# Attention in a hybrid diffusion step: key sums taken in the columns of the output, divisions on output rows

## The chip, the cores and the metric

The kernel runs on one core of a Trainium2 chip. The metric is device time in microseconds for one launch. The engines named below are TensorE (PE; its weight loads are listed apart as PEld), VectorE (DVE), ScalarE (ACT), GpSimd (POOL) and SyncE (SP), which issues the DMA transfers. The engines run at the same time and wait for each other through semaphores; each takes its own instructions in order.

## What is computed

The reference is one step of a network of two layers. Each layer projects 1,152 tokens (128 of a prompt, 1,024 of a sample), runs three mixers beside each other, merges them and adds the result to the stream. The change lies in the first mixer, an attention with 8 heads; a key has 64 plain and 32 rotary components, a value 64:

```python
def mla_attention(q_nope, q_rope, k_nope, k_rope, v):
    scale = (QK_NOPE + QK_ROPE) ** -0.5
    def block(qs):
        qn, qr = qs
        s = (jnp.einsum('bqhd,bkhd->bhqk', qn, k_nope)
             + jnp.einsum('bqhr,bkr->bhqk', qr, k_rope)).astype(jnp.float32) * scale
        pr = jax.nn.softmax(s, axis=-1).astype(v.dtype)
        return jnp.einsum('bhqk,bkhd->bqhd', pr, v)
    ...
```

The sample's 1,024 queries attend to 1,152 keys (128 of the context and their own 1,024), the prompt's 128 queries to 128 keys. All data are 32-bit floats.

## The kernel before

Most of a layer is put in order by a planner. The attention (`attn_all`, line 1221) is not: its order is written by hand, as a loop over slots. A **group** is one head with 512 of the sample's queries, 16 groups a layer; groups 16 and 17 hold four heads of the prompt each. A **slot** is one block of 128 keys of one group, nine slots a group, one for a prompt group.

- `st` (in a slot): three products give the scores of 128 keys by 512 queries, keys on partitions, in a PSUM tile st. The query tile q has a row 96 with the negated maximum of each query, against a row of ones in K, so that the maximum is subtracted by the product itself. ScalarE takes the exponential into a tile P. GpSimd adds up the nine P of a group in a tile acc.
- `s1`: the maxima are found ahead, some 18 slots before the group. Twelve products s a group (in the prompt four) have 128 queries on partitions and 384 keys in columns, in two PSUM buffers; VectorE takes the maximum of each (mx), and `rows_a` the maximum of three and its negative (nm, 128 x 4). `rows_b` moves nm by DMA into row 96 of q. In the sample, product t takes the queries t, t + 4, t + 8 and so on, so that a partition's four values of nm lie beside each other in the row and one transfer moves them all; in the prompt it takes 128 queries in a row, and there are four transfers.
- `pv`, three slots behind a group's last block: nine value products (tile po), V as weights, 64 columns by 512 queries. Even blocks add up in PSUM partitions 0 to 63, odd ones in 64 to 127, and go through the two column halves of the array. `fin_b` copies one half to SBUF on ScalarE (tile ot), `fin_e` adds the other on VectorE.
- `fin_a`, one slot later: four products with columns t, t + 4, ... of acc as weights and one column of ones give the sum over keys of each query, with queries on partitions (sm, 128 x 4). VectorE takes the reciprocal (rc), and SP stores it to DRAM (Rd). `fin_c` loads it back, spread over 64 partitions (rb), and `fin_d`, seven slots after `pv`, multiplies ot by rb and stores it (oD).
- For the last three groups `fin_a` and `fin_c` go another way: GpSimd multiplies the identity by rc, and a product with ones spreads the row.

Fill tiles (fg), products of a later gate projection, stand in the beginning of the attention, among its last slots and behind it. Behind them begins the merge of the next stage (tile mg).

Of the kernel before, what the change touches and what calls it, by code (L numbers as in the profile page):

```python
# [8 lines left out]
F32 = mybir.dt.float32  # L9
# [258 lines left out]
class Kern:  # L268
# [101 lines left out]
    def run(self, ctx):  # L370
# [21 lines left out]
        self.Rd = dram("Rd", (18, 512))  # L392
# [828 lines left out]
    def attn_all(self, l):  # L1221
# [19 lines left out]
        def prep(i):  # L1241
# [4 lines left out]
            if hh >= 0:  # L1246
# [11 lines left out]
                stores = [(self.oD[0, hh // 2, r64(hh), t0:t0 + 512], slice(0, 512))]  # L1258
            else:
# [17 lines left out]
                stores = [(self.oD[0, 2 * w:2 * w + 2, r64(h), 0:128].rearrange("j p t -> p j t"), h) for h in range(2)]  # L1277
# [76 lines left out]
        def fin_a(i):  # L1354
            d = groups[i]
            sm = self.psm.tile([128, 512], F32, tag="ms", name=f"sm{d['nm']}")
            for t in range(4):
                self.mm(sm[:, t:t + 1], d["acc"][:, t::4], self.ones[:, 0:1])
            r = self.S("rc", d["nm"], 4)
            nc.vector.reciprocal(r, sm[:, 0:4])  # L1360
            nm = f"rb{d['nm']}"
            if i < NG - 3:
                d["rb"] = pt.tile([128, 512], F32, tag="rb", bufs=1, name=nm)
                self.st(self.Rd[i].rearrange("(x t) -> x t", t=4), r)
            else:
                d["rb"] = pt.tile([128, 512], F32, tag="P", bufs=13, name=nm)
                self.tt("p", d["rb"].rearrange("p (x t) -> p x t", t=4), self.ident.unsqueeze(2).to_broadcast([128, 128, 4]),
                        r.unsqueeze(1).to_broadcast([128, 128, 4]), ALU.mult)

        def fin_b(i):  # L1370
            d = groups[i]
            d["t"] = pt.tile([64, 512], F32, tag="ot", bufs=3, name=f"ot{d['nm']}")
            self.cp("a", d["t"], d["po"][0:64, :] if d["prompt"] else d["po"][64:128, :])

        def fin_e(i):
            d = groups[i]
            if not d["prompt"]:
                self.tt("v", d["t"], d["po"][0:64, :], d["t"], ALU.add)

        def fin_c(i):  # L1380
            d = groups[i]
            if i < NG - 3:
                self.ld(d["rb"][0:64], self.Rd[i].unsqueeze(0).to_broadcast([64, 512]))
                d["rb"] = d["rb"][0:64]
            else:

                rb = self.pst.tile([128, 512], F32, tag="st", name=f"rb{d['nm']}")
                self.mm(rb[0:64, :], self.ones[:, 0:64], d["rb"])
                d["rb"] = rb[0:64]

        def fin_d(i):
            d = groups[i]
            self.tt("v", d["t"], d["t"], d["rb"], ALU.mult)
            for dst, c in d["stores"]:
                self.st(dst, d["t"][:, c] if not d["prompt"] else d["t"].rearrange("p (j h t) -> p j h t", j=2, h=2)[:, :, c])
# [3 lines left out]
        F0, RB, FA, LAG, FC, FD, FE = 18, 2, 1, 3, 3, 6, 2  # L1399
# [36 lines left out]

        for i in range(3):
            add(NS + 1 + i, fin_a, NG - 3 + i)
# [49 lines left out]
        for n in range(NS + 14):  # L1488
# [6 lines left out]
            if x:  # L1495
                if x[1] == groups[x[0]]["blocks"] - 1:
                    pv(x[0])
                    add(n + 1, fin_b, x[0])
                    add(n + FE, fin_e, x[0])
                    if x[0] < NG - 3:  # L1500
                        for f, m in ((fin_a, FA), (fin_c, FA + FC), (fin_d, FA + FD)):
                            add(n + m, f, x[0])
                    else:
                        add(n + 1, fin_c, x[0])
                        add(n + 2, fin_d, x[0])
# [812 lines left out]
```

## Time and profile before

| | |
|---|---|
| median of three runs | 3682.22 us |
| lowest and highest | 3678.1 and 3687.41 us |
| the profiled execution | 3702.81 us |
| its span, first to last instruction | 3701.0 us |
| mean granted TensorE clock | 0.957 |
| TensorE, VectorE, ScalarE, GpSimd busy | 96%, 53%, 30%, 38% |

A page lists busy time and instructions for each engine. A timeline row gives the start, the time until the end of the last of the merged instructions, the engine, the source line (L95 and L98 are helpers through which all instructions go, so tiles tell them apart), the operation with its tiles as output<-inputs, and in brackets how long the engine was idle before and what released it. A 32-bit product that is not in the faster 32-bit format counts as two instructions in the trace: four key sums are eight.

### The profile page before, as it was taken

Reading aid. Unit: us, or ns where it says so; the run is one execution under the profiler, and the core shown is the slowest. Engines: PE = TensorE matmul, PEld = TensorE weight load, DVE = VectorE, ACT = ScalarE, POOL = GpSimd, SP = SyncE. Lnnn points to the kernel's source line nnn. Section 1 sums busy time; section 2 is a strip of 40 time slices with the busy share of each in tenths; the row PEclk is TensorE's granted clock in tenths of the full one; section 3 lists DMA queues with packets and bytes.
Section 4 is the critical chain, followed back from the end, with each engine's and each line's share of the span. In section 5 each row is a group of like instructions: output and inputs, shape, how many; then the busy total and the mean of one; then the engine's idle time right before and its main releaser. Section 6 shows DMA issues by size and latency. Waiting matters only on the chain. (4 is left out here: it accounts for less than half of the span.)

```text
span 3701.0 us, 62464 instructions
## 1 busy us (share of the span) xinstructions
PE 3543.0 (96%) x24330; PEld 3080.1 (83%) x24330; DVE 1969.5 (53%) x4492; ACT 1102.2 (30%) x2327; POOL 1396.8 (38%) x1456
## 2 busy tenths in 40 slices
PE   7999999998999999999999999999999999999998
PEld 4988777777876789999999877777887667999998
DVE  4477676755555234541575777776455542131236
ACT  4432222224233222221344232212242332121234
POOL 3165555432266401332122645653323662123311
PEclk8999899999998899999999989999999998999999
DMA  5332212225622133441233222311364222132222
GB/s 184 93 106 74 57 54 72 68 59 171 185 66 67 47 111 113 121 127 52 101 101 95 87 75 79 77 48 55 98 223 117 69 61 67 56 95 61 81 79 88
DMA packets 315207, 336.79 MB, mean 91 GB/s; under 512 B 146208, under 2 KB 231904, under 8 KB 314528
## 3 DMA queue, kind: packets, MB, share of 16 engines
q1 hardware_dynamic: 314912, 332.80, 30.6%
q8 instruction: 192, 3.15, 0.3%
q14 instruction: 103, 0.84, 0.1%
HBM read 240.16 MB, written 92.47 MB: 90 GB/s over the span
## 5 line engine op out<-in xcount | busy, mean ns | idle before, releaser
L98 PE MATMUL ip<-h,wh_wi 128*128 128x384 f32 x5328 | 1167.0, 358 | 2.3 <-DVE gb L98 1.1
L98 PEld LDWEIGHTS ip<-h,wh_wi 128*128 128x128 f32 x5328 | 933.0, 194 | 54.4 <-issue 15.9
L98 PE MATMUL mg<-h,wh_mg 128*128 128x384 f32 x3456 | 623.2, 335 | 2.5 <-ACT mt L98 2.5
L98 PEld LDWEIGHTS mg<-h,wh_mg 128*128 128x128 f32 x3456 | 602.0, 188 | 3.1 <-ACT mt L98 3.1
L95 POOL TENSOR_TENSOR acc<-acc,P 128x512 f32<-128x512 f32 x224 | 290.2, 1295 | 199.7 <-ACT P L95 188.0
L95 DVE TENSOR_REDUCE mx<-s 128x1 f32<-128x384 f32 (+1 forms) x400 | 206.8, 540 | 240.4 <-PE s L95 239.3
L98 PE MATMUL pp<-ob,wp 128*128 128x384 f32 x1728 | 329.2, 341 | 2.3 <-DVE mU L98 1.2
L98 POOL TENSOR_TENSOR tmp<-M,X 128x2 f32<-128x2 f32 (+30 forms) x310 | 217.7, 702 | 277.1 <-DVE X L98 258.2
L98 PEld LDWEIGHTS pp<-ob,wp 128*128 128x128 f32 x1728 | 305.9, 191 | 11.1 <-DVE mt L98 6.6
L95 PE MATMUL st<-q,K 97*128 97x512 f32 (+1 forms) x912 | 290.4, 434 | 0.0
L95 ACT ACTIVATE P<-st 128x512 f32<-128x512 f32 x292 | 174.5, 598 | 351.4 <-PE st L95 314.7
L98 POOL TENSOR_TENSOR wh_mg<-wrm,wh_mg 128x512 fp32r<-128x512 f32 x88 | 117.1, 1333 | 424.0 <-ACT wh_mg L98 353.5
L98 POOL TENSOR_TENSOR mU<-mU,mt 128x384 f32<-128x384 f32 x96 | 108.3, 1128 | 327.2 <-DVE mt L98 327.1
L95 PEld LDWEIGHTS st<-q,K 97*128 97x128 f32 x912 | 185.1, 215 | 42.7 <-issue 24.3
L98 POOL TENSOR_TENSOR wh_wi<-wri,wh_wi 128x512 fp32r<-128x512 f32 x112 | 153.4, 1380 | 160.0 <-ACT wh_wi L98 157.9
L98 PE MATMUL wop<-mh,wh_wo 128*128 128x384 f32 x1152 | 203.6, 336 | 3.4 <-DVE mt L98 3.4
L98 PEld LDWEIGHTS wop<-mh,wh_wo 128*128 128x128 f32 x1152 | 199.8, 188 | 5.1 <-DVE mt L98 4.0
L98 DVE TENSOR_REDUCE X<-tmp 128x1 f32<-128x2 f32 (+30 forms) x620 | 184.5, 319 | 31.3 <-POOL tmp L98 23.4
L98 DVE SCALAR_TENSOR_TENSOR mt<-mt,pp 128x384 f32<-128x384 f32 x96 | 53.1, 553 | 254.5 <-ACT mt L98 239.9
L98 ACT ACTIVATE VT<-pv,sst 128x64 f32<-128x64 f32 x256 | 66.7, 311 | 367.0 <-DVE scr L98 350.7
L98 DVE TENSOR_TENSOR tmp<-M,X 128x2 f32<-128x2 f32 (+30 forms) x310 | 163.0, 526 | 20.9 <-POOL M L98 15.0
L98 ACT ACTIVATE mt<-mg 128x384 f32<-128x384 f32 x144 | 70.3, 488 | 339.9 <-PE mg L98 329.7
(302 smaller groups left out, 5104.5 us busy)
## 6 DMA issues: line engine op xcount, KB each, us to landing
wri<-in_w_in SPq DMA_DIRECT2D x160, 256.0 KB, 3.4
wrm<-in_w_in SPq DMA_DIRECT2D x96, 256.0 KB, 3.0
wada<-in_w_ada SPq DMA_DIRECT2D x64, 256.0 KB, 3.0
or<-oD SPq DMA_DIRECT2D x72, 192.0 KB, 3.0
wrp<-in_w_p SPq DMA_DIRECT2D x48, 256.0 KB, 3.0
gD<-gt SPq DMA_DIRECT2D x48, 192.0 KB, 1.9
KNd<-hl_uk SPq DMA_DIRECT2D x24, 384.0 KB, 3.4
QNd<-hl_uq SPq DMA_DIRECT2D x24, 384.0 KB, 3.7
```

The costliest lines, as they stand in the source:

```text
L95: return real(*a, **kw)
L98: op.f = lambda: real(*a, **kw)
```

## The change

- The four products for the key sums become two, behind the value products in `pv`: 64 columns of ones as weights, 256 queries of acc in columns. The first writes PSUM partitions 0 to 63, the second 64 to 127, so that each sum stands on 64 partitions, in the place of the output row that it divides.
- The output tile ot becomes 128 x 256: queries 0 to 255 on partitions 0 to 63, queries 256 to 511 on 64 to 127. Copies and additions are made in two halves; there are two stores a group.
- `fin_d` takes the reciprocal of 128 x 256 in PSUM and multiplies. It is called just before the next group's `pv`; for the last three groups two slots after their own.
- `fin_a`, `fin_c`, the tile in DRAM and GpSimd's products with the identity are gone.
- The two halves for value blocks are swapped: even blocks now use partitions 64 to 127.
- Product t of the maxima takes 128 queries in a row also in the sample; `rows_b` makes four transfers for every group.

```diff
-            ts = slice(t * 128, t * 128 + 128) if d["prompt"] else slice(t, 512, 4)
+            ts = slice(t * 128, t * 128 + 128)
 def rows_b(i):
-            if d["prompt"]:
-                for t in range(4):
-                    self.ld(row[:, t * 128:t * 128 + 128], mr[:, t:t + 1])
-            else:
-                self.ld(row, mr)
+            for t in range(4):
+                self.ld(row[:, t * 128:t * 128 + 128], mr[:, t:t + 1])
 def pv(i):
-            for b in range(n if n > 1 else 0):
-                self.mm(po[b % 2 * 64:b % 2 * 64 + 64, :], Vs[i][:, b], d["P"][b], b < 2, b > n - 3)
+            else:
+                for b in range(n):
+                    h = (b + 1) % 2 * 64
+                    self.mm(po[h:h + 64, :], Vs[i][:, b], d["P"][b], b < 2, b > n - 3)
+            if i < NG - 2:
+                d["sm"] = self.psm.tile([128, 512], F32, tag="ms", name=f"sm{d['nm']}")
+            else:
+                d["sm"] = self.pst.tile([128, 512], F32, tag="st", name=f"sm{d['nm']}")
+            for h in range(2):
+                self.mm(d["sm"][h * 64:h * 64 + 64, 0:256], self.ones[:, 0:64], d["acc"][:, h * 256:h * 256 + 256])
-        def fin_a(i):
-            for t in range(4):
-                self.mm(sm[:, t:t + 1], d["acc"][:, t::4], self.ones[:, 0:1])
-            nc.vector.reciprocal(r, sm[:, 0:4])
-            if i < NG - 3:
-                self.st(self.Rd[i].rearrange("(x t) -> x t", t=4), r)
-            else:
-                self.tt("p", d["rb"]..., self.ident..., r..., ALU.mult)
...
 def fin_b(i):
-            d["t"] = pt.tile([64, 512], F32, tag="ot", bufs=3, name=f"ot{d['nm']}")
-            self.cp("a", d["t"], d["po"][0:64, :] if d["prompt"] else d["po"][64:128, :])
+            t, po = pt.tile([128, 256], F32, tag="ot", bufs=3, name=f"ot{d['nm']}"), d["po"]
+            self.cp("a", t[0:64], po[0:64, 0:256] if d["prompt"] else po[64:128, 0:256])
+            self.cp("a", t[64:128], po[0:64, 256:512])
 def fin_e(i):
-                self.tt("v", d["t"], d["po"][0:64, :], d["t"], ALU.add)
+                self.tt("v", t[0:64], po[0:64, 0:256], t[0:64], ALU.add)
+                self.tt("v", t[64:128], po[64:128, 256:512], t[64:128], ALU.add)
 def fin_d(i):
-            self.tt("v", d["t"], d["t"], d["rb"], ALU.mult)
+            nc.vector.reciprocal(sm, sm)
+            self.tt("v", t, t, sm, ALU.mult)
 main loop, at a group's last block, three slots behind
+                    if 0 < i < NG - 2:
+                        fin_d(i - 1)
                     pv(x[0])
```

On TensorE, from the last value product of group 1 on, before (po value products, st scores, s products for the maxima, sm key sums; the numbers in names are those of group, block and buffer):

```order
L95 MATMUL po_1_10625<-P_1_8_10576,V_0_10151 64x512
L95 MATMUL st_2_3_10635<-q_2_10046,K_1_10049 128x512 x3
L95 MATMUL s_4_4_10642<-K_2_10050,q_0_10044 128x384
L95 MATMUL s_4_5_10645<-K_2_10050,q_0_10044 128x384
L95 MATMUL sm_1_10650<-cst,acc_1_1_10473 128x1 x4
L95 MATMUL st_2_4_10659<-q_2_10046,K_1_10049 128x512 x3
```

The same place on TensorE after the change:

```order
L95 MATMUL po_1_10633<-P_1_8_10579,V_0_10150 64x512
L95 MATMUL sm_1_10643<-acc_1_1_10478,cst 64x256 x2
L95 MATMUL st_2_3_10646<-q_2_10045,K_1_10048 128x512 x3
L95 MATMUL s_4_4_10653<-K_2_10049,q_0_10043 128x384
L95 MATMUL s_4_5_10656<-K_2_10049,q_0_10043 128x384
L95 MATMUL st_2_4_10662<-q_2_10045,K_1_10048 128x512 x3
```

The sums moved ahead of a slot's scores and of two products for the maxima, right behind the value products.

On VectorE, around the value products of group 1, which TensorE starts after product s_4_3, before:

```order
L95 TENSOR_SCALAR nm_3_10589<-mx_3_10234 128x4
L95 TENSOR_REDUCE mx_4_10465<-s_4_0_10591 128x1
L95 TENSOR_REDUCE mx_4_10465<-s_4_1_10594 128x1
L95 TENSOR_TENSOR ot_0_10514<-ot_0_10514,rb_0_10523 64x512
L95 TENSOR_REDUCE mx_4_10465<-s_4_2_10611 128x1
L95 TENSOR_REDUCE mx_4_10465<-s_4_3_10622 128x1
L95 TENSOR_REDUCE mx_4_10465<-s_4_4_10642 128x1
L95 TENSOR_REDUCE mx_4_10465<-s_4_5_10645 128x1
L95 RECIPROCAL rc_1_10655<-sm_1_10650 128x4
L95 TENSOR_REDUCE mx_4_10465<-s_4_6_10668 128x1
L95 TENSOR_TENSOR ot_1_10648<-po_1_10625,ot_1_10648 64x512
```

The same place on VectorE after the change:

```order
L95 TENSOR_SCALAR nm_3_10592<-mx_3_10236 128x4
L95 TENSOR_REDUCE mx_4_10470<-s_4_0_10594 128x1
L95 TENSOR_REDUCE mx_4_10470<-s_4_1_10597 128x1
L95 TENSOR_REDUCE mx_4_10470<-s_4_2_10612 128x1
L95 TENSOR_REDUCE mx_4_10470<-s_4_3_10626 128x1
L95 RECIPROCAL sm_0_10509<-sm_0_10509 128x256
L95 TENSOR_TENSOR ot_0_10525<-ot_0_10525,sm_0_10509 128x256
L95 TENSOR_REDUCE mx_4_10470<-s_4_4_10653 128x1
L95 TENSOR_REDUCE mx_4_10470<-s_4_5_10656 128x1
L95 TENSOR_REDUCE mx_4_10470<-s_4_6_10671 128x1
L95 TENSOR_TENSOR ot_1_10659<-po_1_10633,ot_1_10659 64x256 x2
```

The multiplication of group 0 moved from between the second and third product of group 4 to behind the fourth, with the long reciprocal ahead of it; the short reciprocal of group 1 left.

## Rows read from the trace of the kernel before

**Rows 1.** The page, busy microseconds, share of the span and instructions, TensorE to GpSimd

```profile
PE 3543.0 (96%) x24330; PEld 3080.1 (83%) x24330; DVE 1969.5 (53%) x4492; ACT 1102.2 (30%) x2327; POOL 1396.8 (38%) x1456
```

**Rows 2.** Stretches: length, busy PE, PEld, DVE, ACT, POOL, granted clock, DMA share, GB/s

```profile
1011.60:1278.90 267.30, 264.13 (x1063) 192.90 (x1062) 122.58 (x241) 92.10 (x156) 157.46 (x121) 0.91 0.28 65
2824.70:3091.36 266.66, 262.20 (x1062) 189.64 (x1061) 123.70 (x242) 92.08 (x156) 159.87 (x121) 0.93 0.27 65
```

**Rows 3.** Timeline of TensorE, value products of the first layer's groups 0 and 13

```profile
1011.57 4.51 PE L95 MATMUL po<-P,V 128*64 128x512 f32 x18
...
1233.18 4.51 PE L95 MATMUL po<-P,V 128*64 128x512 f32 x18
```

**Rows 4.** Timeline of one period without a slow stretch, some rows

```profile
1078.79 4.51 PE L95 MATMUL po<-P,V 128*64 128x512 f32 x18
...
1083.23 0.97 PE L95 MATMUL st<-q,K 97*128 97x512 f32 x3
...
1084.25 1.96 PEld L95 LDWEIGHTS sm<-cst,acc 128*128 128x128 f32 x8
...
1092.16 1.20 DVE L95 TENSOR_SCALAR nm<-mx 128x4 fp32r<-128x4 f32 x1
...
1093.87 0.56 PE L95 MATMUL s<-K,q 96*128 96x384 f32 x1 [0.63 <-DVE mx L95]
...
1095.25 4.50 PE L95 MATMUL po<-P,V 128*64 128x512 f32 x18
```

**Rows 5.** A stretch of one microsecond, and the timeline of scores behind it

```profile
1119.00:1120.00 1.00, 1.00 (x3) 0.87 (x4) 0.18 (x1) 0.00 (x0) 0.22 (x1) 0.56 0.00 0
...
1120.81 1.48 PE L95 MATMUL st<-q,K 97*128 97x512 f32 x3
```

**Rows 6.** Timeline, scores of two slots in a row, twice, at full clock

```profile
1106.74 0.86 PE L95 MATMUL st<-q,K 97*128 97x512 f32 x3
...
1107.62 0.87 PE L95 MATMUL st<-q,K 97*128 97x512 f32 x3
...
1248.31 0.86 PE L95 MATMUL st<-q,K 97*128 97x512 f32 x3
...
1249.19 0.86 PE L95 MATMUL st<-q,K 97*128 97x512 f32 x3
```

**Rows 7.** Groups of VectorE by line and form: busy, mean ns, idle before

```profile
L95 DVE RECIPROCAL rc<-sm 128x4 f32<-128x4 f32 x36 | 6.6, 182 | 68.0 <-PE sm L95 68.0
L98 DVE RECIPROCAL sc<-sc 128x144 f32<-128x144 f32 x2 | 2.1, 1052 | 0.1
...
L95 DVE TENSOR_REDUCE mx<-s 128x1 f32<-128x384 f32 (+1 forms) x400 | 206.8, 540 | 240.4 <-PE s L95 239.3
...
L95 DVE TENSOR_TENSOR ot<-po,ot 64x512 f32<-64x512 f32 x13 | 8.7, 672 | 0.0
```

**Rows 8.** SP's timeline, and DMA issues with KB each and us to landing

```profile
1245.48 2.47 SPq L95 DMA_DIRECT2D q<-nm  x4
...
q<-nm SPq DMA_DIRECT2D x14, 2.0 KB, 2.3
q<-nm SPq DMA_DIRECT2D x8, 0.5 KB, 2.0
```

**Rows 9.** Timeline of TensorE from the value products of group 15 to the merge

```profile
1278.90 4.50 PE L95 MATMUL po<-P,V 128*64 128x512 f32 x18
...
1287.40 1.97 PE L95 MATMUL rb<-rb,cst 128*64 128x512 f32 x2 [1.39 <-POOL rb L95]
...
1289.16 1.91 PE L95 MATMUL po<-P,V 128*64 128x128 f32 x8
...
1305.23 8.63 PE L95 MATMUL fg<-h,wh_wf 128*128 128x384 f32 x44
...
1313.70 21.48 PE L98 MATMUL mg<-h,wh_mg 128*128 128x384 f32 x123
```

More of the change, by code (lines that the diff above doesn't have):

```diff
@@ L391, in run @@
         self.gD = dram("gD", (2, 4, 128, T))
-        self.Rd = dram("Rd", (18, 512))
         nu = lambda j: 32 if j == 4 else 64
@@ L1257, in prep @@
                 blocks = 9
-                stores = [(self.oD[0, hh // 2, r64(hh), t0:t0 + 512], slice(0, 512))]
+                stores = [(self.oD[0, hh // 2, r64(hh), t0 + h * 256:t0 + h * 256 + 256], h) for h in range(2)]
             else:
@@ L1276, in prep @@
                 blocks = 1
-                stores = [(self.oD[0, 2 * w:2 * w + 2, r64(h), 0:128].rearrange("j p t -> p j t"), h) for h in range(2)]
+                stores = [(self.oD[0, 2 * w + j, r64(h), 0:128], (j, h)) for j in range(2) for h in range(2)]
             mx = self.S("mx", nm, 16, 4)
@@ L1350, in pv @@
                     self.mm(po[0:64, c], Vs[i][:, j], d["P"][0][:, c])
-            for b in range(n if n > 1 else 0):
-                self.mm(po[b % 2 * 64:b % 2 * 64 + 64, :], Vs[i][:, b], d["P"][b], b < 2, b > n - 3)
-        def fin_a(i):
-            d = groups[i]
-            sm = self.psm.tile([128, 512], F32, tag="ms", name=f"sm{d['nm']}")
-            for t in range(4):
-                self.mm(sm[:, t:t + 1], d["acc"][:, t::4], self.ones[:, 0:1])
-            r = self.S("rc", d["nm"], 4)
-            nc.vector.reciprocal(r, sm[:, 0:4])
-            nm = f"rb{d['nm']}"
-            if i < NG - 3:
-                d["rb"] = pt.tile([128, 512], F32, tag="rb", bufs=1, name=nm)
-                self.st(self.Rd[i].rearrange("(x t) -> x t", t=4), r)
-            else:
-                d["rb"] = pt.tile([128, 512], F32, tag="P", bufs=13, name=nm)
-                self.tt("p", d["rb"].rearrange("p (x t) -> p x t", t=4), self.ident.unsqueeze(2).to_broadcast([128, 128, 4]),
-                        r.unsqueeze(1).to_broadcast([128, 128, 4]), ALU.mult)
+            else:
+                for b in range(n):
+                    h = (b + 1) % 2 * 64
+                    self.mm(po[h:h + 64, :], Vs[i][:, b], d["P"][b], b < 2, b > n - 3)
@@ L1373, in fin_b @@
-            self.cp("a", d["t"], d["po"][0:64, :] if d["prompt"] else d["po"][64:128, :])
+            t, po = pt.tile([128, 256], F32, tag="ot", bufs=3, name=f"ot{d['nm']}"), d["po"]
+            d["t"] = t
+            self.cp("a", t[0:64], po[0:64, 0:256] if d["prompt"] else po[64:128, 0:256])
+            self.cp("a", t[64:128], po[0:64, 256:512])
         def fin_e(i):
             d = groups[i]
+            t, po = d["t"], d["po"]
             if not d["prompt"]:
-                self.tt("v", d["t"], d["po"][0:64, :], d["t"], ALU.add)
@@ L1380, in fin_c @@
[L1380 to L1384, printed above, removed]
-            else:
-                rb = self.pst.tile([128, 512], F32, tag="st", name=f"rb{d['nm']}")
-                self.mm(rb[0:64, :], self.ones[:, 0:64], d["rb"])
-                d["rb"] = rb[0:64]
+                self.tt("v", t[0:64], po[0:64, 0:256], t[0:64], ALU.add)
+                self.tt("v", t[64:128], po[64:128, 256:512], t[64:128], ALU.add)
@@ L1391, in fin_d @@
         def fin_d(i):
             d = groups[i]
-            self.tt("v", d["t"], d["t"], d["rb"], ALU.mult)
-            for dst, c in d["stores"]:
-                self.st(dst, d["t"][:, c] if not d["prompt"] else d["t"].rearrange("p (j h t) -> p j h t", j=2, h=2)[:, :, c])
+            t, sm = d["t"], d["sm"][:, 0:256]
+            nc.vector.reciprocal(sm, sm)
+            self.tt("v", t, t, sm, ALU.mult)
+            for dst, h in d["stores"]:
+                self.st(dst, t[h[0] * 64:h[0] * 64 + 64, h[1] * 128:h[1] * 128 + 128] if d["prompt"] else t[h * 64:h * 64 + 64])
@@ L1397, in attn_all @@
         at = lambda n: slots[n] if 0 <= n < NS else None
         todo = {}
-        F0, RB, FA, LAG, FC, FD, FE = 18, 2, 1, 3, 3, 6, 2
+        F0, RB, LAG, FE = 18, 2, 3, 2
         def add(n, f, *a):
@@ L1435, in attn_all @@
                 n0 += 1
-        for i in range(3):
-            add(NS + 1 + i, fin_a, NG - 3 + i)
         def head():
@@ L1496, in attn_all @@
                 if x[1] == groups[x[0]]["blocks"] - 1:
[L1497 to L1505, printed above, removed]
+                    i = x[0]
+                    if 0 < i < NG - 2:
+                        fin_d(i - 1)
+                    pv(i)
+                    add(n + 1, fin_b, i)
+                    add(n + FE, fin_e, i)
+                    if i >= NG - 3:
+                        add(n + FE, fin_d, i)
     HB = [slice(0, 64), slice(64, 128)]
```

## Prediction

> **What bounds the kernel now.** I read the page first: TensorE is busy for 96% of the span, VectorE for 53%, GpSimd for 38% [rows 1]. The change touches only the attention, so I asked for its two stretches, from the first value product (the product of the exponentials with V, tile po) of a layer to the last: 267.30 and 266.66 us, TensorE busy for 264 and 262 of them, at a granted clock of 0.91 and 0.93 [rows 2]. So what TensorE does there, and at which clock, sets the time. Then the timeline, to see the beat. A group of 512 queries of one head is one period. The first of the layer's value products starts at 1011.57, the fourteenth at 1233.18 [rows 3]: 13 periods of 17.05 us. The last two periods, with fill tiles among them, take 267.30 - 221.61 = 45.7 us together.
>
> A period without a slow stretch lasts 1095.25 - 1078.79 = 16.46 us. It opens with the nine value products, 1083.23 - 1078.79 = 4.44 us, and holds the four key-sum products, whose weight loads fill 1.96 us (eight instructions, each loading 128 columns to move one), and one place where TensorE waits 0.63 us for VectorE, behind a negation of the maxima (nm) that took 1.20 us [rows 4].
>
> In one-microsecond windows the granted clock drops to half speed (the 1.2 GHz level) in 24 of the 32 periods, each time between one and four microseconds after the key sums began, never behind value products alone. One such window has 0.56, and in that stretch the three score products of a slot take 1.48 us [rows 5] where they take 0.86 at full clock [rows 6]. The mean period is 17.05 - 16.46 = 0.59 us longer than the undisturbed one.
>
> **The change part by part.** *Key sums.* Out: 1.96 us a period. In: two products of a 128 x 64 block of ones with 256 columns each, in the two column halves that the value products use. Eighteen value instructions of 512 columns take 4.44 us, side by side, 0.247 us each [rows 4]; four of 256 columns take 4 x 0.247 / 2 = 0.49 us, or twice that, 0.99, if the halves do not run beside each other, or nothing, if they vanish beside the last value block, which has one half free. I take 0.49, since the order of the halves was turned so that they go on alternating. Gain 1.96 - 0.49 = 1.47 us (0.97 to 1.96).
>
> *Clock.* With the one-column products gone I take the undisturbed period as the base, because the low stretches stand behind them alone: 0.59 us a period (0 to 0.59).
>
> *Max queries in plain order.* Twelve products a period load contiguous columns in place of every fourth. A slot with one such product and three score products runs from 1106.74 to 1107.62, 0.88 us; a slot with a contiguously loaded fill product in its place from 1248.31 to 1249.19, 0.88 us as well [rows 6]. The long load is hidden. I book nothing; the ends are 0 and 12 x 0.1 = 1.2 us, if where two of them follow each other it is the load and not VectorE that holds the second.
>
> *VectorE.* Out, per group: the reciprocal of 128 x 4 (0.18 us), the multiplication by the broadcast row, and an addition of 64 x 512 (0.67 us). In: two additions of 64 x 256 (about 0.4 us each, from the 0.67 with a fixed share of 0.13), a reciprocal of 128 x 256 and one multiplication of 128 x 256. The reciprocal: 1052 ns for 144 elements, 182 for 4 [rows 7], so 6.2 ns an element and 1.05 + 112 x 0.0062 = 1.75 us; the multiplication 0.4. These 2.2 us stand just before the next group's value products, while TensorE is busy for 4.44 us and needs nothing of VectorE. VectorE is by then one or two reductions behind (0.54 us each [rows 7]), so it is done some 3.2 us after the value products start. This is a new wait: the sums have one PSUM buffer, and the next key sums, about 3.95 us in, wait for that multiplication. Behind them in TensorE's queue stand all further scores. With 0.7 us to spare I book nothing; each 0.1 us of lateness would cost 0.1 us. On the other side the 1.96 us of key sums were time in which VectorE caught up with two reductions; now scores follow at once and the max products, with two PSUM buffers, wait sooner. The 0.63 us wait behind nm stays and can grow. Ends: all of the 0.63 goes (-0.6), or one pair of reductions is exposed (+1.1); I take +0.35, nearer to the middle, since the long multiplication leaves this place too.
>
> *Queues.* Out on SP: the store of the reciprocals and their broadcast load. In: three more row loads and one more store a group. Four row loads take 2.47 us of issue and land in 2.0 us, against 2.3 us for the one load of before [rows 8]. They start a value phase and seven slots before the first score that reads the row (4.9 + 7 x 0.88, about 11 us), so 4.8 us are hidden; late, they would cost a microsecond for each microsecond. The two stores now wait on SP for the multiplication; behind them stand loads of V, q and K for groups that begin nine or more slots later. ScalarE copies two halves in place of one tile, 0.1 us more, beside slack.
>
> The Trainium skill (DMA: Bandwidth & Descriptors, Specifications) asks for at least 512 B a transfer at full rate and warns of read-modify-write below; it speaks against rows loaded in pieces of 4 B. The prompt's 0.5 KB loads, which are such pieces, land no later than the 2 KB ones [rows 8], so by the trace it costs nothing, and by the rule it would be the fourth rival below.
>
> *A period:* 16.46 - 1.47 + 0.35 = 15.34, against 17.05: 1.7 us, times 13 = 22 us. In the last two periods TensorE interleaves fill tiles and does not wait for VectorE: 1.47 plus about half of a slow stretch of some 3.5 us, together 3.0 each, 6 us.
>
> *Tail.* Value products of group 15 start at 1278.90, so they end at 1283.34; the merge's first product (mg) starts at 1313.70: 30.4 us. In between TensorE three times waits for GpSimd (1.39 us the first time) and spreads reciprocals with a broadcast product (1.97 us), runs three key sums, and twice does prompt value products at half clock, in 1.91 us [rows 9]. After: 53 fill products at 8.63 / 44 = 0.196 us (10.4), two prompt value products at full clock (2 x 0.95), three key sums (3 x 0.49), and one wait of about 1.2 us, since the last value products reuse the bank that VectorE's additions of group 15 must first have read: 15 us. Gain 15.4 us (11 to 17). The three divisions of VectorE (6.5 us) lie beside the fill; the merge's weights and the first loads of stored outputs come off the same queues, earlier by the same amount.
>
> *Sum.* 22 + 6 + 15.4 = 43.4 us a layer, 87 us for two. The profiled execution took 3702.8 us, so 3616; it was 20.6 us above the median of 3682.2, and the same 87 us off the median gives **3595 us**.
>
> **Rivals.** (1) *The clock stays low.* If the half-array value products set it off as much as the sums, each period keeps 0.59 us, less what VectorE's waits hide in it, and the tail and the filled periods run partly at half clock: 2 x (13 x 0.35 + 3 + 4) = 23 us given back, 3618. Against it: never a drop behind value products alone. The Trainium skill (TensorE: Matmul & The Clock Gate, Part 1) says that the clock follows how busy TensorE recently was; by it either product could be the one, and the trace decides for the sums.
>
> (2) *VectorE becomes the engine that is waited for.* Its work per period is about 12 x 0.54 reductions, 0.8 additions, 2.2 division and up to 1.4 for nm, 10.9 of 15.3 us, and the 2.2 can't be shared with reductions. With +1.1 us of new waits: 13 x 0.95 + 6 + 13 = 31 us a layer, 3620.
>
> (3) *The waits vanish.* nm and the long multiplication leave no wait and the doubled max products go faster: 13 x 2.7 + 6 + 17 = 58 a layer, 3566.
>
> (4) *Slower than before: the row comes late.* If the 512 pieces of 4 B a group took a row longer to land than the 11 us it has, each of 32 groups would stall by the excess; the gain of 87 us is gone when a row needs 11 + 87/32 = 13.7 us, and at 15 us the time is 3595 + 32 x 4 = 3723. The rows land in 2.0 us, so I give it little.
>
> (5) *The sums don't run as said:* halves one after the other, and they wait about 2 us for the division each time: the gain of a period is gone, the tail stays: 3682 - 2 x 15 = 3652; with no gain in the tail either, no change.
>
> **How the numbers follow.** Forecast 0.62 (3575 to 3612), rival (1) 0.12, (2) 0.12, (3) 0.08, (4) 0.02, (5) 0.04 of which 0.02 no change. The range 3563 to 3624 takes in the forecast, (1), (2) and (3), and leaves out about 0.1 at the upper end and a little at the lower. About 0.3% (11 us) is what a measurement of this kernel can tell from no change: faster 0.96, same 0.02, slower 0.02.
>
> **What would show it.** Right: a period near 15.3 us; sum products that take about half a microsecond and begin without a wait; granted clock near 1.00 in both stretches; a VectorE reciprocal of about 1.75 us inside the value products; some 15 us from the end of group 15's value products to the merge. Wrong: TensorE idle ahead of the sums, released by VectorE's multiplication; longer waits of the max products for reductions; low stretches still behind the value products; the first score of a group waiting for its row.

## The result and the profile after

The changed kernel takes 3574.74 us (median of four runs, 3567.19 to 3586.19) against 3684.81 us before. The ratio is 0.9692, with a 95% interval of 0.9657 to 0.9727. That is 110 us less, where 87 were forecast: 3595 was predicted, and the time lies inside the range, just below the forecast's own band (3575 to 3612) and nearer to rival 3's 3566. The profiled execution has a span of 3584.4 us. First its page, busy microseconds, share and instructions by engine, against [rows 1]:

```profile
PE 3426.7 (96%) x24174; PEld 2953.6 (82%) x24174; DVE 2006.8 (56%) x4524; ACT 1106.2 (31%) x2363; POOL 1382.6 (39%) x1450
```

TensorE's share is the same 96%. It does 116 us less, so the time went out of its own work and its pace. The two stretches of [rows 2] show that. Here are the thirteen periods alone, from the value products of group 0 to those of group 13, in each layer of the changed kernel (length, busy PE, PEld, DVE, ACT, POOL, granted clock, DMA share, GB/s):

```profile
1001.44:1187.06 185.62, 180.98 (x797) 111.05 (x796) 124.55 (x237) 81.11 (x147) 134.97 (x105) 1.00 0.32 72
2766.07:2951.95 185.88, 181.15 (x796) 110.96 (x795) 124.69 (x237) 81.06 (x147) 134.93 (x105) 1.00 0.33 72
```

Before, the same thirteen took 221.61 and 222.50 us at a clock of 0.91 and 0.92; now the clock is 1.00. One of the new periods, in rows of its timeline (start, length, engine, operation, tile; in brackets the idle time before it and what ended it), to be laid beside [rows 4]:

```profile
1043.95 4.08 PE L95 MATMUL po<-P,V 128*64 128x512 f32 x17
1047.44 0.59 PE L95 MATMUL sm<-acc,cst 128*64 128x256 f32 x2
1047.86 0.59 PE L95 MATMUL po<-P,V 128*64 128x512 f32 x1
1048.29 0.59 PE L95 MATMUL sm<-acc,cst 128*64 128x256 f32 x2
1048.82 0.96 PE L95 MATMUL st<-q,K 97*128 97x512 f32 x3
...
1053.05 0.45 PE L95 MATMUL s<-K,q 96*128 96x384 f32 x1 [0.24 <-DVE mx L95]
...
1058.05 0.65 PE L95 MATMUL po<-P,V 128*64 128x512 f32 x2
...
1044.53 1.76 DVE L95 RECIPROCAL sm<-sm 128x256 f32<-128x256 f32 x1
1046.32 0.42 DVE L95 TENSOR_TENSOR ot<-ot,sm 128x256 f32<-128x256 f32 x1
```

The period is 14.10 us instead of 16.46. The sums begin beside the last value block and wait for nothing. The next scores start 4.87 us after the value products did, against 4.44 us with no sums between in [rows 4]. VectorE's division ends at 1046.74, 0.7 us before the first sum. The wait behind the negation is gone, and 0.24 us at an earlier place is left. In one period a layer, here 15.57 us long, an instruction of VectorE for weights of the gate projection (weight splitting, 0.71 us) stands just ahead of the negation, and TensorE waits 1.20 us.

The tail of the first layer, TensorE's timeline from the value products of group 15 to the merge, against [rows 9]:

```profile
1226.88 4.08 PE L95 MATMUL po<-P,V 128*64 128x512 f32 x17
...
1231.75 0.97 PE L95 MATMUL fg<-h,wh_wf 128*128 128x384 f32 x4
1232.65 0.98 PE L95 MATMUL po<-P,V 128*64 128x128 f32 x7
...
1234.61 0.98 PE L95 MATMUL po<-P,V 128*64 128x128 f32 x7 [0.44 <-ACT ot L95]
...
1236.06 8.78 PE L95 MATMUL fg<-h,wh_wf 128*128 128x384 f32 x49
1244.68 1.55 PE L98 MATMUL mg<-h,wh_mg 128*128 128x384 f32 x8
```

From 1226.88 to the merge are 17.8 us, 34.8 before. The prompt value products take 0.98 us instead of 1.91, and the three waits for GpSimd have become one of 0.44 us for ScalarE.

By pieces, in us, first and second layer, from the starts of the same instructions in both traces:

| piece | predicted gain | gain, layer 1 | gain, layer 2 |
|---|---|---|---|
| first max product to first value products | none | 2.3 | 1.5 |
| thirteen periods | 22 | 36.0 | 36.6 |
| last two periods | 6 | 5.9 | 4.3 |
| tail to the merge | 15.4 | 17.0 | 17.1 |
| sum | 43.4 | 61.2 | 59.5 |

The span fell by 116.6 us, 4 us less than the two sums. That part lies outside these pieces, in code that the change doesn't touch: 3022.3 us before and 3026.3 us after, and 2994 to 3029 us over the traces of all runs. What is to be explained is the row of the thirteen periods.

### The profile page after: what moved, and what is told of

Read it like the earlier page. It is cut to its first block, busy times and chain, and to the rows that moved or that the text cites. A ratio compares the mean times of both kernels' runs of the same rounds, so it can differ in the third digit from the quotient of the medians.

```text
span 3584.4 us, 62317 instructions
## 1 busy us (share of the span) xinstructions
PE 3426.7 (96%) x24174; PEld 2953.6 (82%) x24174; DVE 2006.8 (56%) x4524; ACT 1106.2 (31%) x2363; POOL 1382.6 (39%) x1450
## 5 line engine op out<-in xcount | busy, mean ns | idle before, releaser
L95 PE MATMUL st<-q,K 97*128 97x512 f32 (+1 forms) x912 | 257.4, 393 | 0.0
L95 PEld LDWEIGHTS st<-q,K 97*128 97x128 f32 x912 | 164.0, 190 | 28.4 <-issue 11.5
```

The costliest lines, as they stand in the source:

```text
L95: return real(*a, **kw)
```

## The experiments

**The clock: wide sums.** The kernel before, its sums moving 128 columns.

```
-                self.mm(sm[:, t:t + 1], d["acc"][:, t::4], self.ones[:, 0:1])
+                self.mm(sm[:, t * 128:t * 128 + 128], d["acc"][:, t::4], self.ones)
...
-            nc.vector.reciprocal(r, sm[:, 0:4])
+            nc.vector.reciprocal(r, sm[:, 0:512:128])
```

> The kernel before, its four key-sum products moving 128 columns of ones instead of one: the same 128-column loads of the accumulated exponentials, 128 times the columns; the sum that is used is the first of each 128. Theory A1 (TensorE's low clock is set off by products that move almost nothing): low stretches vanish from the attention, granted clock 0.98 to 1.00 there, the four products still take about 2 us because their loads set the time, and the time falls by 0.59 x 32, some 15 to 25 us, to about 3665 us. Rival A2 (the loads of 128 columns from strided fp32, however many columns are moved, set it off): clock 0.91 to 0.93 as before, time within 5 us of the one before.

Measured: 3661.91 us, ratio 0.9933 (0.9902 to 0.9965). Its thirteen periods in each layer:

```profile
1006.19:1219.46 213.27, 205.54 (x848) 144.48 (x848) 119.54 (x224) 79.43 (x134) 139.78 (x106) 1.00 0.30 70
2792.72:3007.22 214.50, 205.41 (x848) 144.38 (x847) 120.17 (x224) 79.44 (x134) 141.33 (x106) 1.00 0.30 69
```

With the same weight loads and 128 times the columns the clock is 1.00. Not one of 26 periods has a mean clock below it, where 19 of 26 did before, and nearly every period is 16.45 us. Theory A1 holds: it was the one-column products, and their low clock cost 8.3 and 8.0 us a layer here (221.61 - 213.27, 222.50 - 214.50). Predicted were 13 x 0.59 = 7.7.

**The sums put back into the changed kernel.**

```
+        def one(i):
+            d = groups[i]
+            for t in range(4):
+                self.mm(d["sm"][:, 256 + t:257 + t], d["acc"][:, t::4], self.ones[:, 0:1])
...
                     add(n + 1, fin_b, i)
+                    add(n + 1, one, i)
```

> The changed kernel plus the four one-column products of the kernel before, one slot after the value products, written into columns 256 to 259 of the sums' tile, which nothing reads: the output does not use them. Theory A (the one-column products themselves set off the low clock): 1.96 us a period come back, and with them low stretches behind most of them: mean granted clock of the attention stretch falls from 1.00 to 0.90 to 0.94, mean period 14.3 to about 16.6, time 3575 + 34 x 2.3 = about 3650 us. Rival B (the low clock came from somewhere else that the change removed: the waits for VectorE, or the trip to DRAM): the clock stays at 1.00, the period grows by 1.96 alone, time 3575 + 34 x 1.96 = about 3640 us or less, where VectorE catches up in them.

Measured: 3669.63 us, ratio 0.9948 (0.9930 to 0.9966); that is 95 us above the changed kernel. One period at full clock and the one before it (columns as above), then the sums and the scores behind them in that slower one, and one microsecond of it:

```profile
1043.44:1060.13 16.69, 15.88 (x70) 10.37 (x69) 10.34 (x18) 6.12 (x12) 10.44 (x9) 1.00 0.34 70
...
1025.01:1043.44 18.43, 18.43 (x71) 12.90 (x70) 9.50 (x18) 6.13 (x12) 11.11 (x10) 0.81 0.21 47
...
1031.03 1.86 PE L95 MATMUL sm<-cst,acc 128*128 128x1 f32 x8
1032.75 1.63 PE L95 MATMUL st<-q,K 97*128 97x512 f32 x3
...
1033.00:1034.00 1.00, 1.00 (x3) 0.81 (x4) 0.00 (x0) 0.00 (x0) 0.00 (x0) 0.50 0.06 16
```

The clock falls at the end of the sums, but in nine of 26 periods and not in most. (A tenth period has a clock below 1.00; there it fell behind a wait of 2.06 us for VectorE.) So the products bring the low clock back, as A says, yet less often than in the kernel before; why less often was not found. The rest of the loss is theirs too: TensorE's busy time in a period at full clock grows from 13.86 to 15.88, about 2.0 us, and the negation waits again (1.02 us).

**The plain order alone, and undone.** The edit in the kernel before; the second experiment is the reverse in the changed kernel.

```
-            ts = slice(t * 128, t * 128 + 128) if d["prompt"] else slice(t, 512, 4)
+            ts = slice(t * 128, t * 128 + 128)
...
-            if d["prompt"]:
-                for t in range(4):
-                    self.ld(row[:, t * 128:t * 128 + 128], mr[:, t:t + 1])
-            else:
-                self.ld(row, mr)
+            for t in range(4):
+                self.ld(row[:, t * 128:t * 128 + 128], mr[:, t:t + 1])
```

> The kernel before with one part of the change alone: the max products take the queries in plain order and four loads write the row; key sums, reciprocals and their trip to DRAM stay as before. Theory A (the plain order gains at the pairs by itself): about 0.4 us a period less, 16.46 to 16.1 in an undisturbed one, and 8 to 15 us in all, to about 3672 us; the granted clock in the two attention stretches still 0.91 to 0.93, since the one-column sums stay. Rival B (it is worth nothing, as the prediction booked it): period 16.46, within 4 us of the time before.

> The changed kernel with one part undone: the max products of the context groups load every fourth query again and one load writes the whole row; sums and division stay as changed. Theory A (the waits at the max products went because contiguous loads let the second of two neighbouring products follow sooner, and because nothing delays the negation): the second of a pair takes 0.31 us again instead of 0.19, about four pairs a period, so the undisturbed period goes from 14.10 to about 14.6 us and the time from 3575 to about 3590 us (32 periods of 0.5). Rival B (the plain order is worth nothing, the waits went because the long multiplication by the broadcast row left VectorE): period 14.10, time within 4 us of 3575. In both the granted clock stays at 1.00 in the attention.

Measured: the plain order alone 3672.33 us, ratio 0.9958 (0.9935 to 0.9982); the changed kernel without it 3612.72 us, ratio 0.9786 (0.9755 to 0.9817). Two periods of the first, at full and at low clock, and one of the second:

```profile
1154.82:1169.92 15.10, 15.10 (x66) 10.09 (x65) 8.08 (x19) 5.96 (x10) 9.47 (x8) 1.00 0.41 82
1138.39:1154.82 16.43, 16.43 (x66) 11.39 (x65) 8.12 (x18) 5.97 (x11) 10.41 (x9) 0.90 0.25 58
```

```profile
1045.91:1061.31 15.40, 14.60 (x62) 9.59 (x62) 10.45 (x18) 6.15 (x12) 10.24 (x9) 1.00 0.26 59
```

Both expected too little of a period (0.4 and 0.5 us), and rival B falls in both. At full clock the plain order is worth 16.46 - 15.10 = 1.36 us a period in the kernel before and 15.40 - 14.10 = 1.30 us in the changed one. The thirteen periods of each layer, in the first kernel and then in the second:

```profile
990.48:1203.58 213.10, 211.42 (x848) 144.27 (x847) 108.90 (x225) 79.32 (x134) 139.22 (x106) 0.92 0.31 70
2783.64:2997.53 213.89, 211.87 (x848) 143.48 (x847) 109.55 (x225) 79.43 (x134) 138.36 (x106) 0.92 0.31 70
...
1000.69:1202.66 201.97, 190.96 (x797) 125.08 (x796) 135.59 (x236) 81.73 (x147) 135.03 (x106) 0.99 0.28 66
2780.46:2981.24 200.78, 191.00 (x796) 125.27 (x795) 134.40 (x236) 81.74 (x147) 134.95 (x106) 0.99 0.28 66
```

In the kernel before, the plain order gains 8.5 and 8.6 us a layer in them, about half of 13 x 1.36, since 19 of 26 periods still fall into the low clock. Undone in the changed kernel it costs 16.4 and 14.9 us, and another 2.3 and 1.3 us ahead of the first value products. In the kernel before, a period with a low stretch was mostly 16.7 to 17.2 us and is about 16.5 with the plain order: the low stretch had hidden VectorE's wait, and what the plain order takes away is in part that hidden wait.

**Wide sums and plain order together.** Both edits above in the kernel before.

> The kernel before with two single parts together: the max products in plain order (with four row loads), and the four key-sum products moving 128 columns of ones, of which one sum each is used. The period of e2 without a slow stretch was 15.10 us, that of e4 with wide sums 16.45 us in every period. Theory A (the plain order is worth 1.35 us a period, and in e2 the lower clock behind the one-column sums took most of it back): every undisturbed period is 15.10 us, granted clock 1.00 in both attention stretches, and the time is that of e4 less 32 x 1.35, some 3662 - 43 = 3619 us. Rival B (the two gains are the same time, taken once): the time stays at 3650 to 3662 us.

Measured: 3640.34 us, ratio 0.9867 (0.9824 to 0.9910). Its thirteen periods:

```profile
996.08:1195.41 199.33, 197.38 (x848) 131.63 (x847) 106.60 (x225) 79.32 (x134) 139.15 (x106) 1.00 0.33 75
2788.18:2989.44 201.26, 199.21 (x848) 132.16 (x847) 105.65 (x225) 79.31 (x134) 139.49 (x106) 0.99 0.33 74
```

The undisturbed periods are 15.10 to 15.14 us, as A says, and the two gains more than add: the wide sums alone took 8.3 and 8.0 us off a layer, the plain order alone 8.5 and 8.6, and both take 22.3 and 21.2, which is 13.9 and 13.2 below the wide sums alone. One of the 26 periods has a clock of 0.90; it comes behind a wait of 1.24 us for VectorE. The 43 us of the expectation had counted all 32 periods. The gain applies in the thirteen, 27 us in both layers, and the medians differ by 22. This kernel stands half-way between before and after: before, less the clock (8.3, 8.0), less the plain order (13.9, 13.2), and from here to the changed kernel another 13.7 and 15.4 for the shorter sums with all that VectorE does differently.

**Where the plain order gains.** The strided kernel, without the negation; below it, the same edit in the changed kernel.

```
+            nm = d["mr"] = self.S("nm", d["nm"], 4, 2, F32R)
...
-                nc.vector.tensor_reduce(out=d["mx"][:, 12:16], in_=d["mx"][:, 0:12].rearrange("p (t k) -> p t k", k=3),
+                nc.vector.tensor_reduce(out=nm, in_=d["mx"][:, 0:12].rearrange("p (t k) -> p t k", k=3),
                                         axis=AX.X, op=ALU.max)
-                m = d["mx"][:, 12:16]
-            nm = d["mr"] = self.S("nm", d["nm"], 4, 2, F32R)
-            nc.vector.tensor_scalar(out=nm, in0=m, scalar1=-1.0, scalar2=None, op0=ALU.mult)
...
-                    self.cp("v", t[96:97, 0, z * CH:z * CH + CH], self.ones[96:97, 0:1].to_broadcast([1, CH]))
+                    self.cp("v", t[96:97, 0, z * CH:z * CH + CH], self.ones[96:97, 0:1].to_broadcast([1, CH]), -1.0)
```

> The kernel of e1 (changed kernel with strided max queries and one row load) without the negation nm: the ones row of the keys is -1 instead, and the last reduction over the three maxima writes the row's source itself. Theory A (in e1 the negation waits on VectorE until the GpSimd addition that is running ends, 1.09 us in place of 0.17, and the max products wait 0.55 us for VectorE behind it): nm's time is gone, the 0.55 us wait too, period 15.40 to about 14.85 us, time 3612.7 - 32 x 0.5 = about 3596 us. That leaves 0.75 of the plain order's 1.30 us a period to the strided loads themselves. Rival B (VectorE's backlog as a whole makes the wait): period stays within 0.15 of 15.40.

> The changed kernel without the negation nm: the ones row of the keys is -1, and the last reduction over the three maxima writes the row's source itself. Theory A (in the changed kernel the negation starts just behind the end of a GpSimd addition in all but a few periods, takes 0.17 us and holds up nobody): undisturbed period 14.10 as before, only the two periods with weight splitting on VectorE (15.57 us) get shorter, by up to 1.1 us each; time 3575 - 2 = 3573, not to be told from 3575. Rival B (each instruction less on VectorE shortens the wait of 0.24 us that is left): 13.9 us a period, time about 3568 us.

First what the negation does. GpSimd's and VectorE's timelines of the strided kernel (e1) around it, with the max product that waits behind it:

```profile
1058.09 1.29 POOL L95 TENSOR_TENSOR acc<-acc,P 128x512 f32<-128x512 f32 x1
...
1058.29 1.12 DVE L95 TENSOR_SCALAR nm<-mx 128x4 fp32r<-128x4 f32 x1
...
1059.92 0.57 PE L95 MATMUL s<-K,q 96*128 96x384 f32 x1 [0.55 <-DVE mx L95]
```

and the same place of the changed kernel:

```profile
1056.12 1.30 POOL L95 TENSOR_TENSOR acc<-acc,P 128x512 f32<-128x512 f32 x1
...
1056.10 0.17 DVE L95 TENSOR_SCALAR nm<-mx 128x4 fp32r<-128x4 f32 x1
```

In the first the negation comes 0.20 us after a GpSimd addition has begun, and ends at 1059.41, 0.03 us after that addition (1059.38). In the kernel before it was the same: an addition from 1092.05 to 1093.34, and the negation of [rows 4] from 1092.16 to 1093.36. In the changed kernel it starts 0.02 us ahead of the addition and takes 0.17 us. The lead is 0.01 to 0.06 us in 24 of its 26 periods, all but the two with weight splitting. The Trainium skill (SBUF — State Buffer, SBUF: two separate sides) says that VectorE, in some of its modes, and GpSimd share a port pair under an exclusive lock, and that the one that starts second waits for the other's whole instruction. These rows agree with it.

Measured: the strided kernel without the negation 3593.73 us, ratio 0.9744 (0.9708 to 0.9780), the changed kernel without it 3568.15 us (3562.46 to 3584.65), ratio 0.9680 (0.9639 to 0.9722). One period of the strided kernel without it, then one of the other and its period with weight splitting:

```profile
1041.53:1055.99 14.46, 14.21 (x63) 9.60 (x62) 9.42 (x17) 6.13 (x12) 10.20 (x9) 1.00 0.24 57
```

```profile
1051.72:1065.80 14.08, 13.84 (x63) 8.49 (x62) 9.42 (x17) 6.11 (x12) 10.20 (x9) 1.00 0.38 83
...
1079.90:1094.38 14.48, 14.10 (x62) 8.57 (x61) 10.53 (x19) 6.61 (x14) 11.03 (x9) 1.00 0.44 100
```

Without the negation the strided period is 14.46 us, 0.94 less and not 0.55: from the scores ahead of the max product that had waited to that product are now 0.70 us instead of 1.41, and from it to the next scores 0.18 instead of 0.42. The changed kernel stays at 14.1 and only its split period falls, from 15.57 to 14.48, as A says. So of the plain order's 1.30 us some 0.94 is the negation, which now falls just ahead of a GpSimd addition, and 0.36 (14.46 - 14.10) is the loads. That the plain order moves the negation there is shown; by which steps it does so is not. At four places of a period, three of which are max products in pairs, the next scores start 0.35, 0.21, 0.29 and 0.40 us after them with contiguous loads, and 0.41, 0.27, 0.41 and 0.51 us with strided ones, 0.35 us in sum. In the other slots with one max product, such as those of [rows 6], nothing changes.

**The tail alone.** The kernel before, with the new sums, two-half outputs and divisions where `i >= NG - 3` (here the sums' part of the edit).

```
+            if i >= NG - 3:
+                p, g = (self.psm, "ms") if i < NG - 2 else (self.pst, "st")
+                d["sm"] = p.tile([128, 512], F32, tag=g, name=f"sm{d['nm']}")
+                for h in range(2):
+                    self.mm(d["sm"][h * 64:h * 64 + 64, 0:256], self.ones[:, 0:64], d["acc"][:, h * 256:h * 256 + 256])
```

> The kernel before, with the new key sums, two-half outputs and divisions in the last three groups of each layer alone (the last context group and the two prompt groups); the fifteen other context groups of a layer keep one-column sums, the DRAM trip and strided max queries. Theory A (the tail's gain stands by itself, because what goes are three waits for GpSimd, three broadcast products and a half-speed clock there): from the start of the last context group's value products to the merge 17 to 19 us instead of 34.8, time before less 2 x 16 to 17, about 3655 us. Rival B (a good part of the tail's gain needs the earlier groups to be done earlier, so that the three divisions and the copies do not queue behind VectorE's older work): 22 us or more in that place, time 3665 us or above.

Measured: 3650.75 us, ratio 0.9909 (0.9877 to 0.9942), 40 us below the runs of before beside it. Its tail on TensorE:

```profile
1256.47 4.08 PE L95 MATMUL po<-P,V 128*64 128x512 f32 x17
...
1264.19 0.98 PE L95 MATMUL po<-P,V 128*64 128x128 f32 x7 [0.43 <-ACT ot L95]
...
1274.24 2.07 PE L98 MATMUL mg<-h,wh_mg 128*128 128x384 f32 x11
```

17.8 us, the changed kernel's own value, while the periods ahead of it stay at 16.45 and more. The tail's gain stands by itself.

**The division among the slots.**

```
-                    if 0 < i < NG - 2:
-                        fin_d(i - 1)
                     pv(i)
                     add(n + 1, fin_b, i)
                     add(n + FE, fin_e, i)
-                    if i >= NG - 3:
-                        add(n + FE, fin_d, i)
+                    add(n + (FE if i >= NG - 3 else 4), fin_d, i)
```

> The changed kernel with one thing moved: a group's division (reciprocal of 128 x 256 and its multiplication, 2.2 us of VectorE) stands four slots behind its own value products, among the score slots, in place of just before the next group's value products. Theory A (the division is free only because it lies beside 4.9 us in which TensorE needs nothing of VectorE): in the slots VectorE then has twelve reductions of 0.54, 0.85 of additions, 0.3 of the last maxima and 2.2 of division, 9.9 us of work in 9.2 us, and the max products have two buffers; they wait 1 to 2 us more in every period: 15.1 to 16.1 us against 14.10, time 3575 + 26 to 52 us, about 3610 us. Rival B (VectorE is busy for 9.5 of 14.1 us, so it catches up wherever the division stands): period within 0.3 us of 14.10, time within 8 us of 3575.

Measured: 3617.82 us, ratio 0.9799 (0.9766 to 0.9832), 33 us above the changed kernel run beside it (3585.29). VectorE's reciprocal and the max product that then waits:

```profile
1059.85 1.75 DVE L95 RECIPROCAL sm<-sm 128x256 f32<-128x256 f32 x1
...
1062.59 0.91 PE L95 MATMUL s<-K,q 96*128 96x384 f32 x2 [0.79 <-DVE mx L95]
```

The period is 15.40 us, 1.30 more. The first two of each layer take 17.6 to 17.8 us, with a wait of 1.88 us for VectorE and a low clock behind it, and the last with fill tiles takes 26.1 us instead of 21.6. Theory A holds: the same 2.2 us of VectorE cost nothing beside the value products and 1.3 us among the scores.

**Rows in smaller pieces.**

```
-            for t in range(4):
-                self.ld(row[:, t * 128:t * 128 + 128], mr[:, t:t + 1])
+            for t in range(8):
+                h = t % 2 * 64
+                self.ld(row[:, t * 64:t * 64 + 64], mr[h:h + 64, t // 2:t // 2 + 1])
```

> The changed kernel with the row of the maxima written by eight loads of 64 pieces of 4 B instead of four loads of 128: the number of DMAs and of issues doubles, the bytes stay. Theory A (a row has some 11 us from its loads to the first score that reads it, and they land 2 to 3 us after issue): no first score of a group waits for its row, period 14.10, time within 4 us of the changed kernel. Rival B (SP's queue or the pieces are near their limit): TensorE waits for the row at the first score of a group, period above 14.3 us, time up by 5 us or more.

Measured: 3602.18 us (3577.93 to 3618.32), ratio 0.9756 (0.9700 to 0.9812). No first score in the thirteen periods waits for its row; the loads land 1.8 us after issue in the median (2.5 us with four). Behind them a prompt group's scores do wait for the row, 0.76 and 0.85 us, so rival B comes true there. Yet the profiled period is 15.24 us, and neither theory foresaw why. VectorE's and GpSimd's timelines at the negation, with the max product behind it:

```profile
1057.05 1.29 POOL L95 TENSOR_TENSOR acc<-acc,P 128x512 f32<-128x512 f32 x1
...
1057.22 1.14 DVE L95 TENSOR_SCALAR nm<-mx 128x4 fp32r<-128x4 f32 x1 [0.24 <-DVE mx L95]
...
1058.88 0.44 PE L95 MATMUL s<-K,q 96*128 96x384 f32 x1 [0.88 <-DVE mx L95]
```

The negation starts 0.24 us later than its predecessor would let it, comes 0.17 us behind the start of the addition and ends with that. The trace shows what holds it: before it overwrites nm, VectorE waits for the semaphores of all earlier loads from that buffer. With eight loads that takes four semaphore instructions of its sequencer, about 0.10 us from one to the next, and the negation starts, in most periods, 0.21 to 0.24 us after the reduction ahead of it. With four loads it takes two, and the negation starts 0.04 us after the reduction. So the pieces cost 1.1 us a period through VectorE's queue, by taking away a lead of 0.02 us. Why two of the four runs are at 3578 and 3588 us and two near 3617 wasn't settled.

**The additions one slot later.**

```
-                    add(n + FE, fin_e, i)
+                    add(n + (3 if i < NG - 3 else FE), fin_e, i)
```

> The kernel of e6 (changed kernel without the negation) with the two additions of an output's halves one slot later, three slots behind the group's value products instead of two. Theory A (the wait of 0.24 us that is left in a period comes from the 0.85 us of additions, which stand ahead of the reductions where two max products follow each other; one slot later they stand behind these): the wait shrinks below 0.1 us, period 13.85 to 14.0 us, time 3568 - 2 to 6 us. Rival B (it only moves to the next pair): period 14.1 us or more, time 3568 us or above.

Measured: 3574.87 us, ratio 0.9689 (0.9660 to 0.9718), undisturbed period 14.05 to 14.10. Theory A falls, and rival B comes nearer, though the period isn't above 14.1; the wait is 0.20 us at the next place:

```profile
1054.57 0.44 PE L95 MATMUL s<-K,q 96*128 96x384 f32 x1 [0.20 <-DVE mx L95]
```

**The changed kernel again.**

> The changed kernel once more, as it is, beside the three above on the same chip, so that they have it to stand against. If the period of 14.10 us and the granted clock of 1.00 in the attention belong to the kernel and not to one execution, both come again, and 15.57 us in the two periods with weight splitting; time 3567 to 3586 us.

Measured: 3585.29 us (3582.85 to 3597.33), ratio 0.9722 (0.9692 to 0.9752). The periods come again (undisturbed 14.05 to 14.11, with splitting 15.57 and 15.59, clock 1.00). The median is 11 us higher, but the profiled execution, with 3582.85 us, is faster than the one above with 3586.19, so what sets the medians apart no trace shows. The changed kernel without the negation is the fastest that was run, but its interval overlaps this one's, so that it beats the changed kernel isn't shown.

## Why the prediction was right, and where it was not

**What bounds the kernel:** right. TensorE's work and clock in the attention set the time, and both gave way.

**Key sums, 1.96 to 0.49 us:** right. The new ones move the next scores by 4.87 - 4.44 = 0.43 us, and the old ones put back take about 2.0 us of TensorE.

**Clock, 0.59 us a period, 7.7 a layer:** right in cause and size, 8.3 and 8.0 with the wide sums. Rival 1 is refuted: behind the new sums none of 26 periods has a clock below 1.00. What the step missed is that this price held only while VectorE's wait hid in the low stretch. With the wait gone a low stretch costs 16.43 - 15.10, 1.3 us a period, and the wide sums then take off 13.8 and 12.6 us a layer.

**Plain order, booked at nothing, ends 0 and 1.2 us:** this step failed. The argument compared two slots with one max product each and was right for those [rows 6]; but a period has places where two follow each other, and there the strided load shows, 0.36 us in all.

**VectorE, the 0.63 us wait "stays and can grow", +0.35 us:** this step failed too, and by more. With strided queries the period is 15.40 us, and 15.34 was the sum. In the changed kernel the wait behind the negation is gone, the end that had been named for it ("all of the 0.63 goes"), worth 0.94 us a period. The step took the wait for VectorE's load; it is a meeting of the negation with a GpSimd addition, and the plain order moved it. The trace of the kernel before had the sign: in its 26 periods the negation takes anything from 0.17 to 1.21 us, and the prediction went by one of them.

Rival 2 is refuted, the waits left are 0.24 us (and 1.20 with weight splitting). Rival 3, "the waits vanish", at a chance of 0.08, is what happened: it gave 2.7 us a period and 58 a layer, and 2.8 and 60 to 61 were measured. The time lies in the range because the range took this rival in; in that it is luck. That the division lies free beside the value products was right, with 0.7 us to spare as worked out, and costs 1.3 us elsewhere.

**Queues and rows:** right, the rows came in time in both layers. The Trainium skill's rule on transfers below 512 B (DMA: Bandwidth & Descriptors, Specifications) shows no cost in the landing of these rows, 2.5 us with four loads and 1.8 us with eight. Rival 4 is refuted for four loads; with eight a prompt group waits some 0.8 us a layer.

**Last two periods and tail:** 6 us forecast, 5.9 and 4.3; 15.4 forecast, 17.0 and 17.1, within its bounds of 11 to 17 but for 0.1. Rival 5 is refuted: the sums wait for nothing. The 2.3 and 1.5 us ahead of the first value products had no term. They are the plain order's too: that stretch is 38.0 and 37.2 us in the kernel before, 35.7 in both layers with the plain order alone, and 38.0 and 37.0 again when it is undone.

So the direction and the terms for the sums, the clock, the division and the tail held. The shortfall of the sum is 17.8 and 16.1 us a layer. From the first max product to the merge, the changed kernel with strided queries takes 18.7 and 16.3 us a layer more than the changed kernel, so the plain order accounts for it, the loads and the vanished wait together. That kernel gains 42.5 and 43.1 us a layer on the kernel before, and 43.4 were forecast. The shares depend on the order in which the parts are taken.

## What to carry to other kernels

When an access pattern is declared free because its load is hidden, look at every neighbourhood in which the instruction stands, above all where two follow each other. A short VectorE instruction that once took 0.17 us and elsewhere 1.2 has met something: look at GpSimd's row beside it before calling it VectorE's load, and take the instruction away if another can do its work, since its price moves with every change of pace. Gains that share a wait don't simply add (8.3 and 8.5 us alone, 22.3 together, in the first layer here); measure one with the other already taken. And a gain that rests on one instruction starting 0.02 us ahead of another can go with the next edit, as it did with eight loads.

## What the runs showed of the hardware

- Eight products that move one column after loading 128 are followed by half clock in 19 of 26 periods; the same loads moving 128 columns in none of 26, and behind them in none of another 26 with the plain order.
- Idleness is followed by it as well: in the strided kernel's period with weight splitting TensorE waits 2.18 us for VectorE, and the clock falls just behind it. A row of its timeline and one microsecond after it:

```profile
1107.78 0.57 PE L95 MATMUL s<-K,q 96*128 96x384 f32 x1 [2.18 <-DVE mx L95]
...
1109.00:1110.00 1.00, 1.00 (x5) 0.46 (x5) 0.08 (x1) 0.34 (x1) 0.00 (x0) 0.50 0.00 0
```

- A negation of 128 x 4 takes 0.17 us or as long as the GpSimd addition beside it still has to run, up to 1.28 us; a reduction with the same output took 0.15 to 0.17 us throughout.
